# A gated linear unit on one core: the closing barrier of the program replaced by a last wait on SyncE

## The chip, the cores and the metric

One core of a Trainium2 chip. The metric is the time of one execution in device microseconds, on the slowest core (there is one). The granted clock was 1.00.

## The reference

```python
def setup_inputs():
    return {"x": np.random.randn(8192, 8192).astype(np.float32)}

def reference(x):
    a, b = np.split(x, 2, axis=-1)
    return a * (1 / (1 + np.exp(-b)))
```

256 MiB are read, 128 MiB are written, and each output element needs one sigmoid and one product.

## The kernel before

The body: 32 tiles of 256 rows in two slots, loads from SyncE's queue, the sigmoid on ScalarE, the product on VectorE, stores from ScalarE's queue. The last tile is worked off in four pieces with a store each.

```python
    for i in range(n_tiles):
        ...
        load = nc.sync.dma_start(out=xs[i % SLOTS], in_=x_t[i])
        ...
            sig = nc.scalar.activation(out=b, in_=b, func=SIG)
            mul = nc.vector.tensor_mul(out=packed[:, r, c], in0=rows[:, r, 0, c], in1=b)
            ...
            if i == n_tiles - 1 and k > 0:
                store(chunks[k - 1])
        store(chunks[-1] if i == n_tiles - 1 else slice(0, R * half))
```

The part that the change touches is the end of the program. The framework closes a program with two barriers of all engines around a clearing of semaphores. This kernel had already rewritten that into one:

```python
def _one_closing_barrier(nc):
    ...
    drain1, gather1, release1, reset, clear, drain2, gather2, release2 = pool
    ...
    landings = sorted(waits.sync_info.on_wait, key=lambda w: w.id == last)
    pool_waits = [ ...one GpSimd event for each w in landings... ]
    block[:] = arrive_and_leave + [drain1, gather1, *pool_waits, reset, clear, drain2, release1]
```

Three words first. A semaphore is a counter that instructions and transfers raise and that instructions wait for. A drain is an instruction that ends once its engine's own work is over (VectorE's took 2.33 us here, beside a last product of 2.28 us). An event (EVENT_SEMAPHORE) only waits for a semaphore or changes one.

Read as a story: PE, ScalarE, VectorE and SyncE drain and report to GpSimd (arrive), then each stands in an event until GpSimd lets it go (leave). GpSimd takes the four reports (`gather1`), waits for all the last transfers with the final store's landing as the last of them, drains, clears the program's semaphores, drains, and releases the four (`release1`).

## Time and profile before

| | before |
|---|---|
| time, median of the first three runs | 934.44 us (934.38 to 934.63) |
| time of the profiled execution | 933.96 us |
| its span, first to last own instruction | 932.03 us |
| last landing in that span | 931.534 us |

The time is 1.93 us longer than the span. The span holds the program's own instructions; what the runtime does before and after them isn't in it. The chain that ended last is the stream of loads and what hangs on it (shares of the span by engine, then by line):

```profile
DMA 73%; DVE 15%; ACT 12%; issue 0%; ACTq 0%
DMA x_sb<-in_x_dram 73%; DVE o_sb L69 15%; ACT x_sb L68 12%; ACTq L62 0%; ACTq L68 0%
```

The chain ends with the last product at 925.7 and doesn't name the closing line at all.

### The profile page before, as it was taken

The page shows a single profiled execution, that of the slowest core. Times are in us where ns is not written, and L with a number is a line of the kernel's source. Part 1 is how long each engine was busy: PE and PEld are TensorE (multiplying, and loading weights), DVE is VectorE, ACT ScalarE, POOL GpSimd, SP SyncE. Part 2 cuts the span into 40 slices and gives each one's busy share as a digit, 9 for nine tenths or more (in the row PEclk, how much of TensorE's full clock was granted, in tenths as well). Part 3 has the DMA queues.
Part 4 walks back from the last instruction along what each step waited for, and adds up shares of the span by engine and source line. Part 5 has one row for each costly group of instructions (what it writes and reads, how often), then busy time and mean ns, then how long its engine had stood idle before and what let it go on. Part 6 is the DMA issues. An engine that isn't in the chain of part 4 may idle for free.

```text
span 932.0 us, 250 instructions
## 1 busy us (share of the span) xinstructions
DVE 278.6 (30%) x38; ACT 227.0 (24%) x39; POOL 0.2 (0%) x4
## 2 busy tenths in 40 slices
DVE  0333213333123331233312333123331233312333
ACT  1323331133311333113331133311333203332033
POOL 0000000000000000000000000000000000000000
DMA  9999999999999999999999999999999999999999
GB/s 405 428 450 428 428 450 405 450 428 428 450 428 428 428 458 419 428 435 465 428 405 456 422 450 428 425 453 405 450 428 428 450 423 432 428 447 430 428 428 405
DMA packets 9649, 402.67 MB, mean 432 GB/s; under 512 B 1072, under 2 KB 1072, under 8 KB 1072
## 3 DMA queue, kind: packets, MB, share of 16 engines
q1 hardware_dynamic: 4608, 268.44, 66.6%
q10 hardware_dynamic: 5040, 134.22, 33.4%
q14 instruction: 1, 0.01, 0.0%
HBM read 268.44 MB, written 134.22 MB: 432 GB/s over the span
## 4 chain that ended last, share of the span: by engine, by line
DMA 73%; DVE 15%; ACT 12%; issue 0%; ACTq 0%
DMA x_sb<-in_x_dram 73%; DVE o_sb L69 15%; ACT x_sb L68 12%; ACTq L62 0%; ACTq L68 0%
## 5 line engine op out<-in xcount | busy, mean ns | idle before, releaser
L69 DVE TENSOR_TENSOR o_sb<-x_sb 128x8192 f32<-128x8192 f32 (+1 forms) x38 | 278.6, 7344 | 647.0 <-ACT x_sb L68 647.0
L68 ACT ACTIVATE x_sb<-x_sb 128x8192 f32<-128x8192 f32 (+1 forms) x38 | 225.7, 5950 | 695.6 <-DMA x_sb<-in_x_dram 694.3
L68 ACT ACT_TABLE_LOAD x1 | 1.3, 1283 | 0.8 <-PEq L162 0.8
L162 POOL MEMSET const-bfloat16-1.0<- 128x1 bf16 x1 | 0.1, 101 | 0.0
L162 POOL MEMSET const-uint8-127<- 128x1 uint8 x1 | 0.1, 101 | 0.0
L162 POOL MEMSET const-float32-0.0<- 128x1 f32 x1 | 0.1, 98 | 0.2 <-issue 0.2
L162 POOL MEMSET const-float32-1.0<- 128x1 f32 x1 | 0.1, 98 | 0.0
## 6 DMA issues: line engine op xcount, KB each, us to landing
out_dram<-o_sb ACTq DMA_DIRECT2D x31, 4096.0 KB, 34.7
out_dram<-o_sb ACTq DMA_DIRECT2D x4, 1024.0 KB, 5.6
x_sb<-in_x_dram SPq DMA_DIRECT2D x32, 42.2
```

The costliest lines, as they stand in the source:

```text
L68: sig = nc.scalar.activation(out=b, in_=b, func=SIG)
L69: mul = nc.vector.tensor_mul(out=packed[:, r, c], in0=rows[:, r, 0, c], in1=b)
L162: nc = _bacc.Bacc("TRN2", target_bir_lowering=False, num_devices=1)
```

## The change

The intent: nobody should wait for anybody at the end. Four engines leave once they have reported, and GpSimd leaves after clearing every semaphore but the final store's, which it can do while that store is still moving. SyncE alone waits for that landing and takes its count back. The runtime must not see the program finished before its last byte has landed, so one engine has to stay.

```diff
-def _one_closing_barrier(nc):
+def _close_on_sync(nc):
...
-    arrive_and_leave = others[: len(others) // 2]
+    arrive = [i for i in others[: len(others) // 2] if i.opcode == "Drain"]
...
-    landings = sorted(waits.sync_info.on_wait, key=lambda w: w.id == last)
+    final = [w for w in waits.sync_info.on_wait if w.id == last]
...
+    for lo, hi in ((reset.reset_range_start, last), (last + 1, reset.reset_range_stop)):
+        if lo < hi:
+            nc.gpsimd.sem_clear(range(lo, hi))
+    clears = block[n:]
...
+    back = mybir.SyncUpdate(... id=last, update_mode="sem-sub-imm", update_value=final[0].wait_value ...)
...
-    block[:] = arrive_and_leave + [drain1, gather1, *pool_waits, reset, clear, drain2, release1]
+    block[:] = [
+        *arrive,
+        drain1,
+        gather1,
+        *(event(POOL, w) for w in waits.sync_info.on_wait if w.id != last),
+        reset,
+        *clears,
+        drain2,
+        event(SP, final[0], [back]),
+    ]
```

More of the change, by code (lines that the diff above doesn't have):

```diff
@@ L117, in _one_closing_barrier, with event @@
     others = [i for i in block[1:] if i.engine != POOL]
-    arrive_and_leave = others[: len(others) // 2]
+    arrive = [i for i in others[: len(others) // 2] if i.opcode == "Drain"]
+    assert len(arrive) == 4
     body = nc.main_func.blocks[1].instructions
     last = [i for i in body if i.engine == ACT and i.opcode == "DMACopy"][-1].sync_info.on_update[0].id
-    landings = sorted(waits.sync_info.on_wait, key=lambda w: w.id == last)
-    pool_waits = [
-        mybir.InstEventSemaphore(
+    final = [w for w in waits.sync_info.on_wait if w.id == last]
+    assert len(final) == 1
+    def event(engine, wait, update=()):
+        return mybir.InstEventSemaphore(
             name=nc.get_next_instruction_name(),
-            engine=POOL,
+            engine=engine,
             debug=waits.debug,
-            sync_info=mybir.SyncInfo(on_wait=[w], on_update=[]),
+            sync_info=mybir.SyncInfo(on_wait=[wait], on_update=list(update)),
         )
-        for w in landings
+    n = len(block)
+    for lo, hi in ((reset.reset_range_start, last), (last + 1, reset.reset_range_stop)):
+        if lo < hi:
+            nc.gpsimd.sem_clear(range(lo, hi))
+    clears = block[n:]
+    assert clears and all(i.opcode == "ISA" for i in clears)
+    back = mybir.SyncUpdate(
+        sync_type="semaphore",
+        id=last,
+        ant_name=final[0].ant_name,
+        update_mode="sem-sub-imm",
+        update_value=final[0].wait_value,
+        update_reg=None,
+    )
+    block[:] = [
[7 more added lines that the diff above has]
+        event(SP, final[0], [back]),
     ]
-    block[:] = arrive_and_leave + [drain1, gather1, *pool_waits, reset, clear, drain2, release1]
 @with_exitstack
@@ L146 @@
     _launch_early(nc)
-    _one_closing_barrier(nc)
+    _close_on_sync(nc)
 _INS = ['x']
```

## The prediction

> **What bounds the kernel now.** I read the page first: its span, the DMA line of the busy slices and the chain that ended last.
>
> ```profile
> span 932.0 us, 250 instructions
> DVE 278.6 (30%) x38; ACT 227.0 (24%) x39; POOL 0.2 (0%) x4
> DMA  9999999999999999999999999999999999999999
> ...
> HBM read 268.44 MB, written 134.22 MB: 432 GB/s over the span
> ```
>
> All sixteen DMA engines are at 90% or more in every one of the 40 slices, while VectorE works 30% and ScalarE 24% of the time. The bytes are 268.44 + 134.22 = 402.66 MB, and 402.66 MB in 932.0 us is the 432 GB/s of the line. So the body is a stream of bytes at the rate that this core gets, and nothing in the change touches one of those bytes, or a load, store, sigmoid or product. Only what comes after the last byte can be saved. The question is how long that is.
>
> So the second view is a table of stretches at the end (stretch, its length, then busy time and count of DVE, ACT and POOL, granted clock, DMA share, GB/s):
>
> ```profile
> 926.00:929.00 3.00, 0.00 (x0) 0.00 (x0) 0.00 (x0) 1.00 1.02 429
> 929.00:930.70 1.70, 0.00 (x0) 0.00 (x0) 0.00 (x0) 1.00 0.97 410
> 930.70:931.50 0.80, 0.00 (x0) 0.00 (x0) 0.00 (x0) 1.00 0.08 31
> 931.50:932.04 0.54, 0.00 (x0) 0.00 (x0) 0.00 (x0) 1.00 0.00 0
> ```
>
> Up to 930.7 the DMA engines are full with the last stores. Then the bytes run out, and in the last 0.54 us nothing moves. The third view is the closing line of the program, in the stretch from 931.5 to the end (engine and operation, count, duration in ns min/median/max, first and last start):
>
> ```profile
> L145 POOLq EVENT_SEMAPHORE  x2: 17/30/43, 931.6 to 931.9; - x2
> L145 POOLq DRAIN  x2: 34/52/70, 931.6 to 931.9; - x2
> L145 POOLq EVENT_SEMAPHORE_RANGE_CLEAR  x1: 93/93/93, 931.7 to 931.7; - x1
> L145 SPq EVENT_SEMAPHORE  x1: 17/17/17, 932.0 to 932.0; - x1
> L145 ACTq EVENT_SEMAPHORE  x1: 17/17/17, 932.0 to 932.0; - x1
> L145 DVEq EVENT_SEMAPHORE  x1: 21/21/21, 932.0 to 932.0; - x1
> L145 PEldq EVENT_SEMAPHORE  x1: 51/51/51, 932.0 to 932.0; - x1
> ```
>
> This is everything that the program does after its last byte: GpSimd takes note of the landing, drains, clears all the semaphores, drains, and releases the four others, which each need one event to leave. The trace's records place them to the nanosecond: the sixteenth increment of the last store's semaphore at 931.534, GpSimd's event from 931.558 to 931.601, drain from 931.645, clear from 931.744, drain from 931.866, the release from 931.929, the four others' events from 931.971 to 931.982, the last of them (PE's, 51 ns) over at 932.033. From the landing to the end: 932.033 - 931.534 = 0.499 us.
>
> The line below is the same source line between 926.04 and 929.5:
>
> ```profile
> L145 POOLq EVENT_SEMAPHORE  x4: 17/43/2604, 926.3 to 926.5; - x4
> L145 ACTq DRAIN  x1: 152/152/152, 926.1 to 926.1; - x1
> ```
>
> GpSimd has all four arrivals at 926.3, as soon as ScalarE, the last to arrive, has issued the last store and drained. One of its events stands until 929.1, the landing of the third of the four last stores. From there only the fourth is missing.
>
> **What the Trainium skill says.** "Runtime: NRT & Kernel Launch", section "The ~15µs preamble/postamble breakdown", puts a barrier, a reset of semaphores and a second barrier of the runtime behind a kernel, some 5 us in all, and gives 44 ns for one hop of such a barrier. Its section "Semaphores 0–2 are reserved" says that the barrier's semaphore is number 2. The trace of before shows them, shorter: semaphore 2 rises nine times between 932.268 and 932.792, then nine times between 933.616 and 934.075, so everything is over 2.04 us after the kernel's end. Most steps of the nine are 34 to 47 ns, which agrees. What matters is one step of the first closing barrier: its third rise comes 205 ns after its second, where the same step at the launch takes 38. Some engine came about 0.17 us late.
>
> "DMA: Bandwidth & Descriptors", "Anatomy of one DMA", says that a DMA's semaphore rises only once its last write is confirmed. Here the last 8 KB packet ends at 931.210 and the semaphore is full at 931.534, 0.32 us later. The change cannot shorten that: somebody still has to wait for it.
>
> "Perfetto Trace Analysis", "Sequencer-only Instruction (DRAIN, etc)", says that a wait for a semaphore lies outside the duration shown. Here it holds for one of two: the event at 931.6 shows 43 ns though GpSimd had stood there since about 929.1; another shows 2604 ns, which is wait. So I judge by when events start and end, not by the sum of their durations.
>
> **The change part by part.** Removed from behind the last landing: GpSimd's event of 43 ns, two drains (70 and 34), a clear (93) and a release (17), which with the gaps between them take the 0.37 us from 931.558 to the start of the release at 931.929; then the release and the others' events, to 932.033. The arrivals of the four other engines at GpSimd stay as they are.
>
> Added: one event on SyncE that waits for the last landing and subtracts the count. GpSimd reacted 24 ns after the sixteenth increment (931.534 to 931.558). An event that also subtracts took 17 ns on SyncE above; I allow up to the 43 ns of GpSimd's. So SyncE should end at 931.534 + 0.024 + 0.017 to 0.043 = 931.575 to 931.601, and the span loses 932.033 less that, 0.43 to 0.46 us.
>
> Moved: GpSimd's clearing, now two clears instead of one because one semaphore in the middle is left out. It needs the other landings alone, so it starts at 929.1. Event, drain, clear and drain took 0.37 us at the end; a second clear adds about 0.12 (the distance from clear to drain, 931.744 to 931.866). It is over by 929.7, 1.8 us before the last landing. It costs nothing, and the release isn't needed.
>
> Behind the span: four engines now reach the runtime's barrier early, and only SyncE comes last. Before, all five left within 0.06 us of each other, and one held the chain up 0.17 us more at its third step. If that one was not SyncE, this wait disappears too. If SyncE stands late in the order, a few more steps of about 40 ns are already done when it comes. I choose 0.15 us, between 0 and 0.35.
>
> Sum: 0.45 + 0.15 = 0.60 us, 934.44 - 0.60 = 933.84. That is 0.06% of the time.
>
> **Rivals.** First: the time doesn't see the end of the program as the trace does, and only the span shrinks, or even nothing that is timed. The profiled execution took 933.96 us with a span of 932.03, so 1.93 us lie outside it, about as much as the runtime's close. For it: where the clock stops isn't shown anywhere. Against it: the close waits for all engines, so an earlier last engine must bring it forward. Span alone: 934.44 - 0.45 = 934.0; nothing: 934.4.
>
> Second: engines that leave early start the runtime's code while the last stores are still moving. If they fetch instructions for it by DMA, that takes a slot from a store: the only such packet within the span of before (8 KB, on queue 14) took 309 ns on its engine, and that engine would land up to 0.31 us later. For it: ScalarE and VectorE now leave at about 926, five microseconds of full DMA before the end. Against it: the trace of before has no packet on that queue near its end, so that code seems to be there already. Time: 934.1 to 934.2.
>
> Third: the chain of the runtime's barrier was held up by SyncE itself, so that the barrier gains nothing from the other four. Time: 934.0. And a gain of 2% (19 us) has no place to come from: the whole tail from the last packet to the end of the runtime's close is 934.075 - 931.210 = 2.9 us.
>
> **Range and chances.** The size of the gain is uncertain by 0.3 us either way (0.3 to 0.9 us). The three timed runs lie within 0.25 us (934.38 to 934.63), but the profiled execution took 933.96, so single executions stray by half a microsecond. Together: 933.2 to 934.4. A change of 2% either way would need something that no view shows; I leave one in a hundred to each side,, for another state of the chip.
>
> **What would show it right or wrong.** Right: a span about 0.45 us shorter relative to the landing, that is, the last event on SyncE within 0.07 us of the sixteenth increment of the last store (0.50 us before); GpSimd's two clears around 929.5, before the last landing; no leaving events on VectorE, ScalarE and PE at all; the runtime's barrier without the 205 ns step; the stores at the same 0.97 to 1.02 DMA share. Wrong: packets on queue 14 among the last stores, a later landing, SyncE's event much longer than 43 ns, or a barrier of the runtime that starts no earlier. I would also be wrong if the loads and stores ran at another rate: 1 us is 0.1% of 432 GB/s, more than all this change is worth.

## The result, and the profile after

| | before | changed |
|---|---|---|
| time, median of 6 runs | 934.30 us (934.06 to 934.63) | 933.13 us (933.10 to 933.31) |
| profiled execution | 933.96 us | 933.10 us |
| its span | 932.03 us | 931.72 us |
| time less span, profiled execution | 1.93 us | 1.38 us |

The medians differ by 1.17 us, twice what was predicted, and 933.13 lies just under the range (933.2 to 934.4). The ratio is 0.9988 with an interval of 0.9975 to 1.0001 (a ratio is the mean time of one kernel's fast runs over that of the other's of the same rounds, so it isn't quite the ratio of the medians that I quote). The interval reaches 1, but the slowest of the six changed runs is 0.75 us below the fastest of the six before. It is "the same" by the 2% rule, as predicted.

The page of the changed kernel has the same stream and the same number of instruction fetches by DMA (queue 14) as before, one:

```profile
span 931.7 us, 247 instructions
DMA packets 9649, 402.67 MB, mean 432 GB/s; under 512 B 1072, under 2 KB 1072, under 8 KB 1072
q14 instruction: 1, 0.01, 0.0%
```

The last stretches of the changed kernel (stretch, length, busy time and count of DVE, ACT, POOL, clock, DMA share, GB/s), to be held against those of before:

```profile
926.00:929.00 3.00, 0.00 (x0) 0.00 (x0) 0.00 (x0) 1.00 1.03 434
929.00:930.70 1.70, 0.00 (x0) 0.00 (x0) 0.00 (x0) 1.00 0.94 400
930.70:931.50 0.80, 0.00 (x0) 0.00 (x0) 0.00 (x0) 1.00 0.23 92
931.50:932.00 0.50, 0.00 (x0) 0.00 (x0) 0.00 (x0) 1.00 0.00 0
```

The bytes run out at about the same place, a little later: 0.23 of the DMA engines are busy from 930.7 to 931.5 instead of 0.08. The landing is at 931.690, where before it was 931.534. So the stream gained nothing here. It lost 0.16 us. The prediction names a later landing as a sign of being wrong, but a second trace of the kernel before (told below) has its landing at 931.909, so this is within what the stream strays by from run to run.

The closing line of the changed kernel, from 929.2 to 930.0 (line 137 is the clearing, line 171 all the rest):

```profile
L171 POOLq EVENT_SEMAPHORE  x2: 43/1344/2646, 926.6 to 929.3; - x2
L171 POOLq DRAIN  x2: 34/52/70, 929.4 to 929.7; - x2
L137 POOLq EVENT_SEMAPHORE_RANGE_CLEAR  x2: 53/59/65, 929.5 to 929.6; - x2
```

and from 930.0 to the end:

```profile
L171 SPq EVENT_SEMAPHORE  x1: 17/17/17, 931.7 to 931.7; - x1
```

The clearing is over at 929.73, about 2 us before the landing, and one event of 17 ns on SyncE is all that is left after it. The program's own end is as the prediction drew it. Now the parts that no span shows. The trace records the changes of the semaphores (a few records are missing), the runtime's barrier among them: semaphore 2 rises nine times in each of two passes after the program, with a reset of the semaphores in between. Counted from the last landing, in us:

| | before | changed | gain |
|---|---|---|---|
| landing to the program's last end | 0.499 | 0.034 | 0.465 |
| from there to the ninth rise (first pass over) | 0.759 | 0.300 | 0.459 |
| ninth to tenth rise (reset of semaphores) | 0.824 | 0.829 | -0.005 |
| tenth to eighteenth rise (second pass) | 0.459 | 0.361 | 0.098 |
| landing to the eighteenth rise | 2.541 | 1.524 | 1.017 |

The metric moves with all of it. From the program's first instruction to the eighteenth rise are 934.075 us before and 933.214 changed; the times of the same executions are 933.96 and 933.10, both 0.11 to 0.12 less. And the sum closes: 1.017 less the later landing, 0.156, is 0.861; the two times differ by 0.86.

So the span's part came as predicted (0.465 for 0.45), and the part behind it was 0.55, not 0.15. The steps of the first pass suggest why. In us after the landing:

```
before    1: 0.734  2: 0.768  3: 0.973  4: 1.018  5: 1.041  6: 1.138  7: 1.177  8: 1.211  9: 1.258
changed   1: -930.590  2: -5.173  3: -1.437  4: -1.394  5: 0.172  6: 0.215  7: 0.253  8: 0.288  9: 0.334
```

In the changed kernel the first four rises come one by one, each when its engine has left: PE has nothing to do and leaves at the start (first rise), ScalarE's drain ends 0.153 us before the second, GpSimd's last drain ends 0.525 us before the third, the fourth follows at once, and SyncE's event ends 0.138 us before the fifth. It looks like a chain PE, ScalarE, GpSimd, VectorE, SyncE, then back. If so, SyncE as the last engine has only four rises after its own. And in the kernel before, the third rise is late because GpSimd needs over half a microsecond to get there: 0.412 (end of its release) to 0.973 is 0.561. This is read from two traces, and the order is my interpretation. The experiments test it.

### The profile page after: what moved, and what is told of

Read it like the earlier page. It is cut to its first block, busy times and chain, and to the rows that moved or that the text cites. A ratio compares the mean times of both kernels' runs of the same rounds, so it can differ in the third digit from the quotient of the medians.

```text
span 931.7 us, 247 instructions
## 1 busy us (share of the span) xinstructions
DVE 278.7 (30%) x38; ACT 227.1 (24%) x39; POOL 0.2 (0%) x4
## 4 chain that ended last, share of the span: by engine, by line
DMA 73%; DVE 15%; ACT 12%; issue 0%; ACTq 0%
DMA x_sb<-in_x_dram 73%; DVE o_sb L69 15%; ACT x_sb L68 12%; ACTq L62 0%; ACTq L68 0%
```

## The experiments

In what follows an engine's way is the time from the end of its last instruction to its rise of semaphore 2.

**Theory A.** Each engine takes its own fixed way from its last instruction to its step of the runtime's barrier (GpSimd 0.53 to 0.56 us, PE 0.235, ScalarE 0.15, SyncE 0.14), the steps come in the order PE, ScalarE, GpSimd, VectorE, SyncE and back, and the pass takes the latest comer. **Rivals**: the surplus is the stream's scatter (B); any engine kept to the end costs all of it (C); which engine is last doesn't matter (D); the losses of single engines add up (E). I judge by the rises counted from the landing of the same trace, because they are free of the stream's scatter, and then look whether the times agree.

### The kernel before, once more

No edit.

> The kernel before, unchanged, as a null: ratio 1.000 within 0.0005. It gives what was missing of before: span and time of every run. Theory A (the gain lies mostly behind the span, in how the engines reach the runtime's closing barrier): the time is 1.93 us longer than the span in each run, against 1.4 us in the changed kernel. Theory B (the gain over 0.6 us was the stream's own scatter): the time less the span is the same in both kernels, about 1.4 to 1.5, and the spans differ by more than 0.45 us.

Measured: 934.34 us against 934.25 for the shared runs of before, ratio 1.0004 (0.9990 to 1.0018). Time less span was 1.89 to 1.95 in its five runs and 1.88 to 1.98 in nine runs of before on the same chip; in the six runs of the changed kernel it was 1.33 to 1.41. B falls for the larger part: the difference sits behind the span, in every run. But the spans of this kernel went from 932.3 to 933.6, so a median of few runs may carry some tenths of scatter. The trace repeats the first one: ninth rise at 1.256, eighteenth at 2.540.

### GpSimd last, without a release

```diff
 (against the kernel before)
-    block[:] = arrive_and_leave + [drain1, gather1, *pool_waits, reset, clear, drain2, release1]
+    arrive = [i for i in arrive_and_leave if i.opcode == "Drain"]
+    block[:] = arrive + [drain1, gather1, *pool_waits, reset, clear, drain2]
```

> The kernel before without its release: the four others leave on arrival, but GpSimd still waits for the last landing and clears afterwards. Theory A (GpSimd needs 0.53 to 0.56 us from its last instruction to its step of the runtime's barrier, and its step comes third): from the last landing, GpSimd ends at 0.37 us, its step comes at 0.89, the ninth rise of the barrier's first pass at 1.13 to 1.18 (before 1.26, changed 0.33); the time is 0.1 to 0.2 us below before. Theory C (letting the four others go is what brought the gain behind the span): the ninth rise at 0.37 + 0.30 = 0.67, time 0.6 us below before.

Measured: GpSimd ends at 0.365, third rise 0.890, ninth 1.173, eighteenth 2.373. The time was 934.07 us against 934.25. What happens behind the landing (from 931.0 to the end of the span):

```profile
L146 POOLq DRAIN  x2: 34/52/70, 931.9 to 932.1; - x2
L146 POOLq EVENT_SEMAPHORE  x1: 43/43/43, 931.8 to 931.8; - x1
L146 POOLq EVENT_SEMAPHORE_RANGE_CLEAR  x1: 93/93/93, 932.0 to 932.0; - x1
```

No other engine has an event there: all four are gone, and the gain is only 0.17 of the 1.02 us (0.085 in the first pass, where GpSimd, with no release to give, ends 0.047 earlier and takes 0.525 instead of 0.561 to its step; the rest in the second, whose slow fourth step is gone). C expected the ninth rise at 0.67. Setting the others free is worth little so long as GpSimd is the last to leave.

### GpSimd alone held back

The changed kernel with one more event on SyncE and one on GpSimd, on a semaphore outside the cleared range:

```diff
 (against the changed kernel; HELD = GpSimd)
+    release = mybir.InstEventSemaphore(... engine=SP, on_update: hold += len(HELD) ...)
...
         event(SP, final[0], [back]),
+        release,
+        *(event(e, go, [one]) for e in HELD),      # go: hold >= 1, one: hold -= 1
```

> The changed kernel, but GpSimd, with its clears done, is held until SyncE has taken the last landing and lets it go. Nothing of the clearing is put back, and three engines leave early. Theory A: GpSimd leaves about 0.15 us after the landing, its step of the barrier comes at 0.70, the ninth rise at 0.93 to 1.00 instead of 0.33; the time is 0.6 us over the changed kernel, 0.5 below before. Theory C: what counts is the serial work taken away and the others' leaving; then it is as the changed kernel, but for 0.1 us.

Measured: GpSimd leaves at 0.149, third rise 0.710, ninth 0.995, eighteenth 2.187. The closing line (from 931.0 on):

```profile
L186 SPq EVENT_SEMAPHORE  x2: 17/17/17, 931.6 to 931.7; - x2
L186 POOLq EVENT_SEMAPHORE  x1: 17/17/17, 931.7 to 931.7; - x1
```

Three events of 17 ns; the span is longer by 0.115 us behind the landing, and yet the end of everything is 2.187 - 1.524 = 0.663 us later than in the changed kernel. Median 933.70 us, 0.55 below before as A expected, though two of the five runs were at 934.59 and 935.18 with spans of 932.7 and 933.3, the stream's scatter (ratio 0.9999). Time less span was 1.88 to 1.96: holding GpSimd alone brings the 1.9 us of before back.

### The other three held back

The same edit with HELD = PE, ScalarE, VectorE.

> The mirror of the one before: PE, ScalarE and VectorE are held until SyncE has taken the last landing, GpSimd leaves early. Theory A: PE needs 0.235 us from its last instruction to the first step, so that the first step comes at 0.42 and the ninth at 0.74 to 0.78 (changed 0.33); the time is 0.4 to 0.45 us over the changed kernel and clearly less than with GpSimd held. Theory C: the whole gain behind the span is lost, ninth rise at 0.9 or later, and the time is above that with GpSimd held.

Measured: first rise 0.424, ninth 0.780, eighteenth 2.067.

```profile
L186 SPq EVENT_SEMAPHORE  x2: 17/17/17, 931.7 to 931.8; - x2
L186 ACTq EVENT_SEMAPHORE  x1: 17/17/17, 931.8 to 931.8; - x1
L186 DVEq EVENT_SEMAPHORE  x1: 21/21/21, 931.8 to 931.8; - x1
L186 PEldq EVENT_SEMAPHORE  x1: 51/51/51, 931.8 to 931.8; - x1
```

A had said 0.42 and 0.74 to 0.78. Three engines held cost 0.54 us and GpSimd alone 0.66, so C falls here too. A's forecast for the time was missed: it had said 0.4 to 0.45 us over the changed kernel and clearly less than with GpSimd held, and the median came 0.64 over, and above GpSimd's. With spans that stray by a microsecond the medians can't tell these two apart (933.77 and 933.70); the traces can, and so can time less span plus what the program does after the landing: 1.77 + 0.19 = 1.96 here, 1.90 + 0.15 = 2.05 with GpSimd held.

### All four held back

The same edit with HELD = all four.

> The changed kernel with all four other engines held until SyncE has taken the last landing. The clearing stays early. Theory A (the barrier's chain takes the latest comer, so that losses don't add up): the third step comes at 0.71 us after the landing and the ninth at 1.00, as with GpSimd held alone (0.995), not later. VectorE leaves late here too, as in the kernel before and with the three held, where one step of the second pass took 0.146 us instead of 0.043: I expect it again, so that the eighteenth rise comes at 2.29 (before 2.54, changed 1.52). Theory E (each engine held adds its own loss): 0.66 and 0.45 us add up, the ninth rise at 1.4.

Measured: third rise 0.710, ninth 0.995, eighteenth 2.280. From its third rise on, the first pass is, to the nanosecond, that of GpSimd held alone. E falls: the pass takes the latest comer. The second pass has the slow fourth step again (0.147 us). The median was 934.28 us against 934.20, where the expected eighteenth rise would put it 0.25 below; the four spans went from 931.9 to 933.3, so this median settles nothing. Time less span was 1.96 to 2.00, and with the 0.187 from landing to end 2.17 against 1.94 + 0.50 = 2.44 before: 0.27 less, as the traces say (2.541 - 2.280 = 0.261).

This run splits the gain in two: clearing early first is worth 0.261 us, and then not holding the four 2.280 - 1.524 = 0.756. The split depends on the order. Where the four were set free first (GpSimd last, without a release), that was worth 0.168, and the rest of the change, early clearing with SyncE as the last, 2.373 - 1.524 = 0.849. Since the pass takes the latest comer, neither part has a worth of its own.

### Another engine as the last

The changed kernel, with the final wait on another engine than SyncE:

```diff
 (against the changed kernel)
-        event(SP, final[0], [back]),
+        event(POOL, final[0], [back]),     # then ACT, PE, DVE in its place
```

> The changed kernel, but GpSimd, its clears done, waits for the last landing and takes it back, not SyncE. Nothing serial is added behind the landing. Theory A: GpSimd's step comes 0.56 us after its event, at 0.60, the ninth rise at 0.89 (changed 0.33), the eighteenth at 2.08; 0.56 us over the changed kernel by the trace. Theory D (one last engine without work behind it is as good as another): as the changed kernel, ninth rise at 0.33.

> The same with ScalarE as the last. Theory A (ScalarE needs 0.15 us to its step, the second of the chain, and seven more follow): step at 0.19 to 0.22, ninth rise at 0.51 to 0.55, eighteenth at 1.70 to 1.74, without the slow step of the second pass. Theory D: ninth rise at 0.33.

> The same with PE as the last, which has the first step of the chain and needs 0.235 us to it: step at 0.30, ninth rise at 0.66, eighteenth at 1.85, without the slow step of the second pass. Theory D: ninth rise at 0.33.

> The changed kernel with VectorE as the engine that waits for the last landing. Theory A: VectorE has the fourth step of the chain, five rises are left after its own; with 0.15 to 0.2 us to its step, the ninth rise comes at 0.42 to 0.50. Theory F (VectorE, when it leaves at the end, comes about 0.1 us late to the second pass, as in the kernel before, with three held and with all held, and in no other): the fourth step of the second pass takes 0.146 us and the eighteenth rise comes 1.28 us after the ninth. Theory G (that step needs several engines leaving at the same time): it takes 0.043 us, 1.19 us after the ninth.

Each has one short event behind the landing. The closing lines of GpSimd's, ScalarE's, PE's and VectorE's run, in this order (from 931.0 on; GpSimd's landing came at 932.986, so that its drain lies about 2 us before it):

```profile
L171 POOLq DRAIN  x1: 34/34/34, 931.0 to 931.0; - x1
L171 POOLq EVENT_SEMAPHORE  x1: 17/17/17, 933.0 to 933.0; - x1
```

```profile
L171 ACTq EVENT_SEMAPHORE  x1: 17/17/17, 931.5 to 931.5; - x1
```

```profile
L171 PEldq EVENT_SEMAPHORE  x1: 51/51/51, 932.2 to 932.2; - x1
```

```profile
L171 DVEq EVENT_SEMAPHORE  x1: 21/21/21, 931.8 to 931.8; - x1
```

Measured, in us after the landing, with the changed kernel for comparison (its second run, told below, in brackets):

| last engine | its event ends | its step (which rise) | way | ninth | eighteenth | median time |
|---|---|---|---|---|---|---|
| SyncE | 0.034 (0.034) | 0.172 (5th) | 0.138 | 0.334 (0.335) | 1.524 (1.525) | 933.13 (933.26) |
| VectorE | 0.048 | 0.245 (4th) | 0.197 | 0.485 | 1.783 | 933.57 |
| ScalarE | 0.038 | 0.179 (2nd) | 0.141 | 0.502 | 1.692 | 933.38 |
| PE | 0.079 | 0.314 (1st) | 0.235 | 0.670 | 1.860 | 933.68 |
| GpSimd | 0.041 | 0.602 (3rd) | 0.561 | 0.886 | 2.085 | 933.83 |

D falls: with nothing else changed, the choice of the last engine moves the end by up to 0.56 us. In each run the rise that came first after the landing has the number that A gave to that engine, and the ones before it had come before the landing (in ScalarE's run the first rise, in VectorE's the first three). Theory A's numbers hold to 0.02 us; ScalarE came a little earlier than I had said (0.179 for 0.19 to 0.22, 0.502 for 0.51 to 0.55). The five medians stand in the order of the eighteenth rise, though neighbours lie within each other's scatter (VectorE's run and the second of the changed kernel ran on another chip than the other three experiments here); before in the same rounds was 934.20 to 934.22.

VectorE's run also settles the 0.1 us of the second pass. Its fourth step took 0.151 us there and the eighteenth rise came 1.298 after the ninth, as F expected. The slow step is in the traces of before, of the three held, of all held and of VectorE last, where VectorE leaves after the landing, and in none of the others (0.043 to 0.044 us in each). What VectorE does in that time no record shows.

### The changed kernel, once more

No edit.

> The changed kernel unchanged: time less span 1.33 to 1.41 in every run, 0.51 to 0.57 below that of before in the same rounds; ninth rise at 0.33 and eighteenth at 1.52 us after the landing; median 0.8 to 1.2 us below before. The stream's own scatter (spans of before went from 932.1 to 933.6) may move the median by 0.3.

Measured: 933.26 us (933.10 to 933.40) against 934.22 (933.96 to 934.28), 0.96 less; ratio 0.9990 (0.9977 to 1.0004). Time less span 1.35 to 1.40, before 1.88 to 1.98. Ninth rise 0.335, eighteenth 1.525. So the trace's 1.02 us is the size of the change, and the 1.17 of the first medians held about 0.15 of scatter. No run beats the changed kernel's end, and none of the experiments points to a better last engine.

## Why the prediction was right or wrong

- **What bounds the kernel: right.** The stream is untouched. Loads, stores and products are the same; the landing moved by no more than its scatter.
- **The program's own tail: right.** 0.43 to 0.46 us were predicted, 0.465 came: SyncE ended 0.034 us after the landing instead of 0.041 to 0.067. (One reading of the working was off without consequence: the five engines left within 0.087 us of each other, from GpSimd's release at 0.412 to PE's end at 0.499, not within 0.06.)
- **GpSimd's clearing costs nothing: right.** It was finished 1.96 us before the landing, and GpSimd's rise came 1.44 us before it. The second clear was cheaper than estimated (the two took 53 and 65 ns).
- **"Behind the span ... I choose 0.15 us, between 0 and 0.35": this step failed.** It measured 0.55, and the mechanism was half seen. I took the 0.17 us for which "some engine" held the chain up as the whole of what could go, and added a few steps. In fact everything up to SyncE's step could go, except SyncE's own short way. From the program's last end, before: PE's way 0.235, a step of 0.034, the wait for GpSimd 0.205, two steps of 0.045 and 0.023, together 0.542 to SyncE's rise. Changed: 0.138. That is 0.404. The four rises back take 0.162 instead of 0.217 (the step after SyncE's is 0.043 instead of 0.097, as VectorE took its own step 1.394 us before the landing; in the passes where VectorE's step came only 0.023 before SyncE's, the step after took 0.097 or more), another 0.055. And the second pass, which I listed and then left out of the sum, gave 0.098 through VectorE. 0.404 + 0.055 + 0.098 - 0.005 = 0.552.
- The numbers that would have led there stood in the trace of before: GpSimd's release ended at 0.412 and the third rise came at 0.973, while PE needed only 0.235. I compared the steps of the pass with those at the launch (the 38 ns are of the second pass there), but not each engine's way to it.
- **First rival (the time sees only the span, or nothing): wrong.** The time runs to the eighteenth rise less 0.11 to 0.12 us, in all eleven other traces and in that of before.
- **Second rival (fetching the runtime's code disturbs the stores): didn't come.** Queue 14 has the same single packet, at 587 us in both traces, far from the last stores.
- **Third rival (the chain was held up by SyncE): the reverse.** SyncE has the fifth place and a way as short as any (0.138 us; ScalarE's 0.141 is no clear difference), which makes it the best engine to be last.
- **The range** was set by a gain of 0.3 to 0.9 us, and the tail's 1.02 us lies outside that, for the step above. The 1.02 us taken from the 934.30 of the six runs is 933.28, inside the range; the stream's scatter took the median to 933.13, 0.07 below it. The chances were right.

## What to carry to other kernels

The end of a program isn't its last instruction: the timed part may include the runtime's closing barrier, and there each engine has its own way and its own place. So ask not only how much work follows the last landing, but which engine is the last to leave, and let it be the one with the shortest way and the fewest steps behind it; here that choice alone was worth up to 0.56 us with no work changed. When a difference of a microsecond is at stake, count from an event inside the same trace: the stream's scatter, over a microsecond at its worst, hid in the medians what the traces showed to the hundredth.

## What the Trainium skill lacked or had wrong

- "Runtime: NRT & Kernel Launch", "The ~15µs preamble/postamble breakdown": it gives closing barrier, reset, and second barrier with the reset of the DMA rings as some 5 us in sum. Here 2.04 us passed from the program's end to the eighteenth rise before, 1.49 changed; no record here separates a reset of the rings, so the two sums needn't cover the same. Its 44 ns for a hop agrees with most steps (34 to 47 ns), but the step after SyncE's took 0.097 us in the pass of before and 0.112 at the launch.
- The same section speaks of a serpentine across five engines with eight hops, which the nine rises here fit, but names no order of engines and no way of each to the barrier. The runs show PE, ScalarE, GpSimd, VectorE, SyncE (the order back wasn't tested on its own), with 0.235, 0.141 to 0.153, 0.525 to 0.561, 0.197 and 0.138 us. GpSimd took 0.525 where a drain was its last instruction and 0.561 where an event was. GpSimd's half microsecond is on no page that I found.
- The same section doesn't say at which point of the closing an execution time ends. Here the time is 0.108 to 0.119 us less than the eighteenth rise, counted from the first instruction, in all twelve traces.
- No page has the late VectorE in the second pass: 0.146 to 0.151 instead of 0.043 us for one step, when VectorE leaves last or among the last.
- "Perfetto Trace Analysis", "Sequencer-only Instruction (DRAIN, etc)", has the wait outside the duration shown. Here events that wait for two semaphores show 2604 ns (before) and 2646 ns (changed) with the wait for the second of them inside, while the last such event of before shows 43 ns though it stood for some 2.4 us.
